# One number of a hand-made order: 16.0 instead of 3.0 matmul-microseconds of projections ahead of the indexer's scores

## The chip, the cores and the metric

The program runs on one core of a Trainium2 chip. The metric is the device time of one execution in microseconds (us). Before the change three runs were timed; one more execution was profiled.

## The reference, cut to what matters

One mixer layer with a mixture of experts, then two layers of a second block; all in float32, on 512 tokens of 1024 features. The change touches the mixer of the first layer alone. There one projection gives the queries of two attentions (`qa`, `qb`), the indexer's queries and key (`qi`, `ki`), keys, values and two gates.

```python
proj = jnp.einsum('bsd,dc->bsc', h, w_in)
qa, ka, va, qi, ki, wi, qb, kvb, gb, gate_a, gate_b = jnp.split(proj, SPLIT_POINTS, axis=-1)
# indexer: eight heads of 32, only tokens it selects are seen by the first attention
idx_logit = jax.nn.relu(jnp.einsum('bthd,bsd->bths', qi, ki))
score = jnp.einsum('bth,bths->bts', wi, idx_logit)
_, sel = lax.top_k(score, k_sel)
o_a = dsa_attention(qa, k, v, sel)                  # softmax over the selected tokens
# second attention: compressed, selected and window branches, weighted by gates
o_b = gc * o_cmp + gs * o_slc + gw * o_win          # queries qb and rope(qb)
merged = jax.nn.sigmoid(gate_a) * (o_a @ w_br_a) + jax.nn.sigmoid(gate_b) * (o_b @ w_br_b)
```

## The kernel before, in words

Matrix products are made of passes on TensorE. A float32 matrix is split into a high and a low part (`wh`, `wl` for weights, `hTh`, `hTl` for the normed tokens), and a step of 128 rows of the contraction is three passes of 512 columns: `hTh,wh`, `hTl,wh`, `hTh,wl`. A product of 128 output columns has eight steps, so 24 passes. The queries `qb` are four products, `qa` four, the gates sixteen.

Weights are fetched by SyncE (a DMA of 512 KB into a raw tile `wr`; line 568 for `qb` and `qa`, line 261 for others), then split: ScalarE writes `wh` (line 242), VectorE or GpSimd `wl` (line 245). A load of `qa` or `qb` serves two products with half of the contraction, so that two loads make two products.

The results of `qb` go through DRAM. `sink` takes a pair of products (two halves of the heads): the pair as it is goes to `d_qn`, and rotated by position (`rope`: four products `t` on VectorE, lines 548 to 551, and a difference and a sum on GpSimd, lines 553 and 554) to `d_qr`. `put` splits each of these four tiles into a high part `sh` (ScalarE, line 534) and a low part `sl` (line 535; VectorE for `d_qn`, GpSimd for `d_qr`) and has SyncE write both (line 540). `sh` and `sl` have two buffers each, so that every third one waits until a write of the tile two before it has landed:

```python
hi = rt.tile([128, T], F32R, tag="sh", name="sh", bufs=2)
lo = rt.tile([128, T], F32R, tag="sl", name="sl", bufs=2)
```

The indexer makes 24 scores (three tiles of tokens, eight heads): a matmul of the index keys `KI` with the index queries `QI` (line 136, as every matmul), a relu `r` on ScalarE (line 779, two buffers) and a weighted sum `sc` on VectorE (lines 781 and 784). `QI` and `KI` are read back from DRAM (lines 637 to 641). Then come `compress` (the products `k_cmp` and `v_cmp`, their blocks `z` against `w1`) and the attentions, sixteen units of a kind and a tile of tokens: S3 W3 C3, S2 W2 C2, S1 W1 C1, S0 W0 C0 of the second attention, D3 D2 D1 D0 of the first (which need the masks `MK` that VectorE makes by `top_k`). Each unit has a part q (scores by query, `KA,QA` and `KC,QB`), a short part b, and a part k (scores by key, `QA,KA`, exponentials, and the sum `po`). Units overlap: part k of one stands behind part q of the next but one.

The order in which all this is emitted is set by `weave`. It walks a chain (indexer, compress, attentions) and takes pieces of a fill (token projections, products of `qb`, of `qa`, of the gates, a step of three passes at a time) between the steps of the chain. The chain can yield a number of microseconds of matmul time as owed to the fill, or a pair (key, lag): then fill is taken until the running sum of matmul time (`self.pe`, 0.425 ns a column, so 0.65 for a step) stands lag behind the moment at which the key was marked. When the chain has ended, what is left of the fill is emitted in one go. The token projections mark the key "tok", and the indexer begins with such a pair:

```python
yield "tok", TUNE["tl0"]
```

The framework's scheduler then lays the instructions out on the engines; each engine runs its own in order, waiting where one isn't ready. SyncE's queue of DMAs is such an order too.

Of the kernel before, what the change touches and what calls it, by code (L numbers as in the profile page):

```python
# [98 lines left out]
    return c  # L99


TUNE = {"mq": 4,"u1":2,"m3":2.0,"m4": 2.0,"m5":1.0,"la":99,"sq2":3.0,"sq":3.0,"fg":2.0,"qt3": 0.5,"bl":2.0,"ee":3,"mk":3.0,"tp":1,"qt1": 1.0,"qt2":1.0,"ws1":1,"ws2":1,"fn": 2.5, "rv": ("qi", "ki"), "tl0": 3.0, "pl": 4.0, "wl": 2.0, "rl": 5.0, "ql": 2.5, "lgm": 8, "shb": 2, "st": 6.0, "sb": 2, "head": 1, "ou": 1, "e2": 3, "p2": 3, "late2": 4, "hv": 0, "pp": 0, "cr": 0, "fp": 2.0, "sh2": 0.0, "mid": 6, "m2": 2.8, "qe": "sync", "y0": {("S", 3): 10.0}, "sh1": 0.5, "cq": 2.5, "o1": [3, 2, 1, 0], "o2": [3, 2, 1, 0], "ix": 0.7, "late": 4, "eb": 3, "ev": 4, "at": 0.5, "tk": 0.0, "tl": 3.0, "obn": 15, "tl2": 1.5, "pf": 3.0, "rx": 4.0, "rs": 6.0, "lo": 16, "lw": 6, "pf0": 2.0, "fx": (0,0,2,0)}


class Kernel:
# [48 lines left out]
    def weave(self, chain, fill, ratio):  # L154
# [14 lines left out]
        for need in chain:  # L169
# [6 lines left out]
            elif need is not None:  # L176
# [8 lines left out]
                owed -= self.pe - p0  # L185
                if TUNE["cr"] == 0 and owed < 0:
                    owed = 0.0
# [70 lines left out]
    def wtile(self, src, kn, cols):  # L258
# [9 lines left out]
        for i in range(0, kn, kn // n):  # L268
            a = slice(i, i + kn // n)
            self.split(hi[:, a], lo[:, a], raw[:, a], hi_eng=eng and (self.nc.vector, None)[TUNE["hv"]], lo_eng=eng)  # L270
        return hi, lo
# [23 lines left out]
    def step(self, k):  # L295
        if k == TUNE["la"]:
            self.due()
# [122 lines left out]
    def first_norm(self, hT, b1, ix):  # L420
# [6 lines left out]
        def load(t):  # L427
            nc.sync.dma_start(xs[t // 2][:, t % 2], I["x"][0, t * 128:(t + 1) * 128])

        def norm(t):  # L430
            x = xs[t // 2][:, t % 2]
            with self.tc.high_priority():
                ss = ix.tile([128, 1], F32, tag="rn_s", name="rn_s", bufs=2)
                nc.scalar.activation(gj[:, 1 + t % 2], x, AF.Square, accum_out=ss)
                rs = self.rstd(ix, ss, 1.0 / D, 1e-6, t == 1)
                nc.vector.scalar_tensor_tensor(x, x, rs, gj[:, 0], op0=OP.mult, op1=OP.mult)
            return lambda: self.to_T(x, hT[0], hT[1], t)

        def rest():
            for t in (2, 3):  # L440
                load(t)
                self.later(TUNE["fn"] * (t - 1), lambda t=t: norm(t)(), t)
        load(0)
# [36 lines left out]
    def mixer1(self, hT):  # L480
# [4 lines left out]
        self.done = {}  # L485
        self.share = TUNE["sh1"]
        pers, pclose = self.pool("b1p")
# [35 lines left out]
        def put(x, n, f, row, rows, ts, scale=None, src0=0, eng=nc.vector):  # L523
# [15 lines left out]
            for x, y in ((0, h), (1, l)):  # L539
                puts.append(self.after(TUNE["pl"], lambda x=x, y=y: nc.sync.dma_start(  # L540
                    DR[n][x, f, row:row + rows, ts], y.bitcast(F32))))
# [1645 lines left out]
```

## Time and profile before

| | us |
|---|---|
| median of three runs | 2065.29 |
| lowest and highest run | 2062.99, 2070.3 |
| the profiled execution's own time | 2065.98 |
| its span, first to last instruction | 2064.2 |
| TensorE busy in it | 1943.5 (94%) |
| longest wait of TensorE | 14.83, ending at 85.32 |
| first matmul of an attention (S3) | 170.76 |
| first matmul of unit D2 | 351.78 |
| last matmul of the attentions | 416.14 |

Times in the trace are microseconds from the span's start. The work around the change lies between 64.84, where the first product of `qb` starts, and some 416, where the attentions end; the remaining three quarters of the span (the merge of the branches, the experts, the second block) come after it and are not touched.

### The profile page before, as it was taken

How to read it: one execution, taken by the hardware profiler on the slowest of the kernel's cores; microseconds unless marked ns; L12 is line 12 of the kernel's file. 1: busy time of each engine (PE TensorE's matmuls, PEld its weight loads, DVE VectorE, ACT ScalarE, POOL GpSimd, SP SyncE). 2: the span in 40 equal slices, each digit the busy share in tenths (PEclk: the TensorE clock that was granted, in tenths of full speed). 3: DMA queues.
4: the chain of work that ended last, by engine and by line, in shares of the span. 5: the costliest groups of instructions: out<-in, count | busy, mean ns of one | idle time of the engine just before them, and what ended most of it. 6: DMA issues, size and time to landing. Idle time of an engine off the chain costs nothing.

```text
span 2064.2 us, 25772 instructions
## 1 busy us (share of the span) xinstructions
PE 1943.5 (94%) x9430; PEld 1521.7 (74%) x9430; DVE 1128.4 (55%) x2034; ACT 844.6 (41%) x1623; POOL 223.1 (11%) x186
## 2 busy tenths in 40 slices
PE   7789989999899998899899999999799999999998
PEld 6667778777555543777778888888687778888886
DVE  8687997664521213687984333335587983333234
ACT  5355657633312112576833222212476833323220
POOL 3143111042000101101020000001001010000001
PEclk9899999999999999899999999999999999999999
DMA  7666433377799995734433333433744334333332
GB/s 188 140 181 147 116 80 103 105 223 275 265 356 395 396 388 183 220 98 128 118 116 111 101 93 102 153 102 108 180 118 128 106 122 150 96 98 96 115 100 71
DMA packets 284495, 328.68 MB, mean 159 GB/s; under 512 B 25562, under 2 KB 206842, under 8 KB 284112
## 3 DMA queue, kind: packets, MB, share of 16 engines
q1 hardware_dynamic: 276912, 306.54, 47.4%
q0 software_dynamic: 7456, 20.49, 3.8%
q8 instruction: 75, 1.23, 0.2%
q14 instruction: 52, 0.43, 0.1%
HBM read 286.63 MB, written 43.38 MB: 160 GB/s over the span
## 4 chain that ended last, share of the span: by engine, by line
PE 52%; DMA 3%; DVE 3%; ACT 2%; issue 1%; POOL 0%; SPq 0%; POOLq 0%; ACTq 0%; DVEq 0%
PE b L136 48%; PE po L136 3%; DVE nm L1891 1%; DMA ks<-bnc 1%; DMA wr<-in_w_in_dram 1%; DMA bnc<-sl 1%; ACT b L1892 1%; PE tp L413 0%; DMA wr<-in_w_o_dram 0%; DMA qs<-bnc 0%; DVE wl L245 0%; DVE pl L245 0%; DMA wr<-in_c_seq_dram 0%; ACT e L1955 0%; ACT wh L242 0%
## 5 line engine op out<-in xcount | busy, mean ns | idle before, releaser
L136 PE MATMUL b<-hTh,wh 128*128 128x512 f32 (+1 forms) x1256 | 477.0, 381 | 7.0 <-ACT wh L242 3.7
L136 PE MATMUL b<-hTh,wl 128*128 128x512 f32 (+1 forms) x1256 | 473.1, 377 | 5.5 <-DVE wl L245 3.4
L136 PE MATMUL b<-hTl,wh 128*128 128x512 f32 (+1 forms) x1256 | 473.6, 377 | 1.7 <-DVE hTl L417 1.7
L242 ACT ACTIVATE wh<-wr 128x1024 fp32r<-128x1024 f32 (+1 forms) x217 | 220.7, 1020 | 561.2 <-PE b L136 332.5
L245 DVE TENSOR_TENSOR wl<-wr,wh 128x1024 fp32r<-128x1024 f32 (+1 forms) x207 | 256.2, 1239 | 340.2 <-ACT wh L242 339.8
L136 PEld LDWEIGHTS b<-hTh,wl 128*128 128x128 f32 x1256 | 240.8, 192 | 50.9 <-DVE wl L245 4.7
L136 PEld LDWEIGHTS b<-hTh,wh 128*128 128x128 f32 x1256 | 241.3, 193 | 50.3 <-ACT wh L242 4.6
L136 PEld LDWEIGHTS b<-hTl,wh 128*128 128x128 f32 x1256 | 241.2, 192 | 41.5 <-DVE hTl L417 3.8
L136 PE MATMUL b<-wl,ah 128*128 128x512 f32 x352 | 137.1, 390 | 0.0
L136 PE MATMUL b<-wh,ah 128*128 128x512 f32 x352 | 137.0, 389 | 0.0
L136 PE MATMUL b<-wh,al 128*128 128x512 f32 x352 | 136.9, 389 | 0.0
L396 POOL TENSOR_TENSOR rs_r<-rs_v,mhalf 128x1 f32<-128x1 f32 x20 | 26.7, 1333 | 781.0 <-DVE rs_v L392 781.0
L245 DVE TENSOR_TENSOR pl<-e,ph 128x512 fp32r<-128x512 f32 x132 | 99.3, 756 | 13.8 <-ACT ph L242 11.4
L1730 DVE TENSOR_TENSOR gs<-b,gs 128x512 f32<-128x512 f32 (+1 forms) x48 | 31.0, 646 | 138.3 <-PE b L136 138.3
L1892 ACT ACTIVATE b<-b,nm 128x512 f32<-128x512 f32 x128 | 84.7, 668 | 23.9 <-DVE nm L1891 23.4
L1891 DVE TENSOR_REDUCE nm<-b 128x1 f32<-128x512 f32 x128 | 82.4, 682 | 18.8 <-PE b L136 18.6
L136 PE MATMUL b<-xr,X 128*64 128x512 f32 x264 | 75.0, 628 | 4.5 <-ACT X L1424 4.5
L136 PEld LDWEIGHTS b<-wl,ah 128*128 128x128 f32 x352 | 66.1, 188 | 13.8
L136 PEld LDWEIGHTS b<-wh,ah 128*128 128x128 f32 x352 | 66.1, 188 | 13.7
L136 PEld LDWEIGHTS b<-wh,al 128*128 128x128 f32 x352 | 66.1, 188 | 13.6
L1955 ACT ACTIVATE e<-b 128x512 f32<-128x512 f32 x128 | 70.6, 616 | 11.5 <-PE b L136 7.4
L245 POOL TENSOR_TENSOR wl<-wr,wh 128x1024 fp32r<-128x1024 f32 (+1 forms) x27 | 55.9, 2073 | 168.3 <-DVE wh L244 80.9
(479 smaller groups left out, 3463.0 us busy)
## 6 DMA issues: line engine op xcount, KB each, us to landing
wr<-in_w_gu_dram SPq DMA_DIRECT2D x88, 512.0 KB
xr<-in_w_gate_up_dram SPq DMA_DIRECT2D x66, 512.0 KB
wr<-in_w_in_dram SPq DMA_DIRECT2D x60, 512.0 KB
wr<-in_w_down_dram SPq DMA_DIRECT2D x44, 512.0 KB
xw<-in_w_gate_up_dram SPq DMA_DIRECT2D x37, 512.0 KB
xy<-in_w_gate_up_dram SPq DMA_DIRECT2D x25, 512.0 KB
xr<-in_w_down_dram SPq DMA_DIRECT2D x24, 512.0 KB
xw<-in_w_down_dram SPq DMA_DIRECT2D x23, 512.0 KB
```

What stands on the lines that cost most here:

```text
L136: self.nc.tensor.matmul(out, a, b, start=start, stop=stop)
L242: nc.scalar.activation(hi, src, AF.Copy)
L245: (lo_eng or nc.vector).tensor_sub(lo, src, hi.bitcast(F32))
L396: nc.gpsimd.tensor_tensor(r, v, self.mhalf, op=OP.pow)
L1730: nc.vector.tensor_mul(g, ps, g)
L1891: nc.vector.tensor_reduce(nm[:, i, r:r + 1], ps, axis=AX.X, op=OP.max, negate=True)
L1892: nc.scalar.activation(ps, ps, AF.Exp, bias=nm[:, i, r:r + 1], accum_out=z[:, i, r:r + 1])
L1955: nc.scalar.activation(e, ps, AF.Exp)
```

## The change

A single entry of the table of numbers changes, and it is used in one place, the line of the indexer shown above:

```diff
-TUNE = {..., "rv": ("qi", "ki"), "tl0": 3.0, "pl": 4.0, ...}
+TUNE = {..., "rv": ("qi", "ki"), "tl0": 16.0, "pl": 4.0, ...}
```

The number is the lag behind "tok". At 0.65 a step, 3.0 is reached in 5 steps and 16.0 in 25; so twenty more steps of `qb`, two and a half products, are emitted ahead of the first score. Since everything else is taken from the fill as before, each later point of the chain stands behind more of the fill, and the fill ends earlier.

What the scheduler makes of it shows in the order on the engines. **First place: TensorE at the first scores.** Before, the first product of `qb` (`b_769`) is followed by three scores, and the second product (`b_809`) is then laid between the scores, one step after each:

```order
L136 MATMUL b_769<-hTh_82,wl_755 128x512
L136 MATMUL b_785<-KI_587,QI_586 128x256
L136 MATMUL b_796<-KI_587,QI_586 128x256
L136 MATMUL b_804<-KI_587,QI_586 128x256
L136 MATMUL b_809<-hTh_82,wh_754 128x512
L136 MATMUL b_809<-hTl_83,wh_754 128x512
L136 MATMUL b_809<-hTh_82,wl_756 128x512
L136 MATMUL b_813<-KI_587,QI_586 128x256
```

Now all four products of `qb` (`b_769`, `b_794`, `b_865`, `b_894`) come first. Behind the last step of the fourth stand seven scores in a row, and then a step of `b_1000`, the first product of `qa`, with weights of `wh_984` and `wl_986`:

```order
L136 MATMUL b_894<-hTh_82,wl_852 128x512
L136 MATMUL b_898<-KI_587,QI_586 128x256
L136 MATMUL b_909<-KI_587,QI_586 128x256
L136 MATMUL b_917<-KI_587,QI_586 128x256
L136 MATMUL b_925<-KI_587,QI_586 128x256
L136 MATMUL b_933<-KI_587,QI_586 128x256
L136 MATMUL b_941<-KI_587,QI_586 128x256
L136 MATMUL b_949<-KI_587,QI_586 128x256
L136 MATMUL b_1000<-hTh_82,wh_984 128x512
L136 MATMUL b_1000<-hTl_83,wh_984 128x512
L136 MATMUL b_1000<-hTh_82,wl_986 128x512
L136 MATMUL b_1004<-KI_587,QI_586 128x256
```

So 72 passes moved from among and behind the scores to a place ahead of them, and the remaining 17 scores now lie among products of `qa`.

**Second place: the writes of `qb` and the first weights of `qa`.** On ScalarE, before, one `sh` of the first product stood ahead of the relus and the next came after ten of them. Now it reads from the sixth relu on (`t_827`, `t_829` and `t_962` are rotated queries, `b_865` and `b_894` the third and fourth product, `wr_988` the first load of `qa`):

```order
L779 ACTIVATE r_943<-b_941 128x256
L779 ACTIVATE r_951<-b_949 128x256
L534 ACTIVATE sh_839<-t_827 128x512
L534 ACTIVATE sh_845<-t_829 128x512
L534 ACTIVATE sh_954<-b_865 128x512
L534 ACTIVATE sh_958<-b_894 128x512
L534 ACTIVATE sh_974<-t_962 128x512
L242 ACTIVATE wh_984<-wr_988 128x512
L242 ACTIVATE wh_985<-wr_988 128x512
```

And on SyncE, after the reads of `KA` and `KC` that stand there in both kernels, the writes and loads are now:

```order
L540 DMA d_qn_178<-sh_819 128x512
L540 DMA d_qn_178<-sl_820 128x512
L540 DMA d_qn_178<-sh_823 128x512
L540 DMA d_qn_178<-sl_824 128x512
L540 DMA d_qr_177<-sh_839 128x512
L540 DMA d_qr_177<-sl_840 128x512
L540 DMA d_qr_177<-sh_845 128x512
L540 DMA d_qr_177<-sl_846 128x512
L540 DMA d_qn_178<-sh_954 128x512
L568 DMA wr_988<-in_w_in_dram 128x4x256
L540 DMA d_qn_178<-sl_955 128x512
L540 DMA d_qn_178<-sh_958 128x512
```

The load `wr_988`, the first of `qa`, stands between the writes of the second pair of `qb`; before, it stood behind all eight writes of `d_qn`, four of `d_qr`, and the loads for `k_cmp`, `v_cmp` and a quarter of `w1`, and TensorE came to the product that needs it later, behind `k_cmp`. The split `wh_984` of `qa` stands behind the seven relus and five of the `sh`.

**Third place: TensorE from D2 to D1.** Before, steps of the gates (`b_3593`) lie between the parts of the units. Here are the last two heads of part q of D2, with a step between them, and its part b:

```order
L136 MATMUL b_3578<-MK2_153,identr_70 128x384
L136 MATMUL b_3593<-hTh_82,wh_3588 128x512
L136 MATMUL b_3593<-hTl_83,wh_3588 128x512
L136 MATMUL b_3593<-hTh_82,wl_3589 128x512
L136 MATMUL b_3597<-KA_144,QA_3518 128x384
L136 MATMUL b_3597<-KC_145,QB_3523 128x384
L136 MATMUL b_3597<-MK2_153,identr_70 128x384
L136 MATMUL b_3603<-identr_70,b20_1438 66x128 x4
```

Now the last gate (`b_3604`) ends ahead of D2, and between the last head, part b and part k of C0 (`KAc`, `KCc` are compressed keys) no step is left:

```order
L136 MATMUL b_3668<-MK2_153,identr_70 128x384
L136 MATMUL b_3677<-KA_144,QA_3608 128x384
L136 MATMUL b_3677<-KC_145,QB_3613 128x384
L136 MATMUL b_3677<-MK2_153,identr_70 128x384
L136 MATMUL b_3683<-identr_70,b20_1547 66x128 x4
L136 MATMUL b_3708<-QA_3355,KAc_164 128x512
L136 MATMUL b_3708<-QB_3360,KCc_165 128x512
L136 MATMUL b_3708<-cmk_162,identr_70 128x512
```

Counted over the whole order, the passes of products that stand ahead of the first matmul of `k_cmp` are 96 before and 153 now; ahead of the first attention 279 and 339; ahead of D2 552 and 624, which is all of them. The fill's last 72 passes, which lay from D2 on, have moved ahead of it.

## Rows read from the trace of the kernel before

**Rows 1.** TensorE's timeline: start, us, engine, line, operation, tiles [idle before <-releaser].
```profile
64.84 0.40 PE L136 MATMUL b<-hTh,wh 128*128 128x512 f32 x1
...
70.10 0.39 PE L136 MATMUL b<-hTh,wl 128*128 128x512 f32 x1
85.32 0.98 PE L136 MATMUL b<-KI,QI 96*128 96x256 f32 x3 [14.83 <-DMA QI<-d_qi]
86.10 0.63 PE L136 MATMUL b<-hTh,wh 128*128 128x512 f32 x1
...
90.58 0.52 PE L136 MATMUL b<-hTh,wh 128*128 128x512 f32 x1
```

**Rows 2.** Windows: us, busy of PE, PEld, DVE, ACT, POOL, PEclk, DMA share, GB/s.
```profile
110.56:170.76 60.20, 53.88 (x224) 41.77 (x225) 43.50 (x67) 26.64 (x43) 30.08 (x23) 0.91 0.67 179
170.76:351.78 181.02, 169.72 (x866) 138.99 (x864) 159.21 (x408) 114.87 (x288) 29.48 (x20) 0.96 0.44 109
351.78:416.36 64.58, 59.97 (x286) 49.32 (x286) 44.07 (x93) 46.26 (x112) 6.78 (x6) 0.92 0.36 104
```

**Rows 3.** TensorE's timeline at k_cmp.
```profile
110.56 0.50 PE L136 MATMUL b<-hTh,wh 128*128 128x512 f32 x1 [1.98 <-ACT wh L242]
...
112.41 0.63 PE L136 MATMUL b<-hTh,wh 128*128 128x512 f32 x1
```

**Rows 4.** ScalarE's timeline: splits of weights, a relu, a split of queries.
```profile
49.34 0.63 ACT L242 ACTIVATE wh<-wr 128x512 fp32r<-128x512 f32 x1 [0.60 <-DMA wr<-in_w_in_dram]
...
92.52 0.38 ACT L779 ACTIVATE r<-b 128x256 f32<-128x256 f32 x1 [0.42 <-PE b L136]
...
104.34 0.62 ACT L534 ACTIVATE sh<-t 128x512 fp32r<-128x512 f32 x1
...
118.43 1.06 ACT L242 ACTIVATE w<-wr 128x1024 fp32r<-128x1024 f32 x1 [2.72 <-DMA wr<-in_w_k_dram]
```

**Rows 5.** VectorE's timeline: a split that waits for a write, a weighted sum, a split.
```profile
52.65 0.86 DVE L538 SCALAR_TENSOR_TENSOR sl<-t,sh 128x256 fp32r<-128x256 f32 x1 [0.57 <-DMA d_k<-sl]
...
88.25 0.48 DVE L781 SCALAR_TENSOR_TENSOR sc<-r,wi,sc 128x256 f32<-128x256 f32 x1 [0.37 <-ACT r L779]
...
95.61 0.69 DVE L535 TENSOR_TENSOR sl<-b,sh 128x512 fp32r<-128x512 f32 x1 [0.18 <-ACT sh L534]
```

**Rows 6.** GpSimd's timeline: rotation and splits of queries.
```profile
97.59 1.29 POOL L553 TENSOR_TENSOR t<-t 128x512 f32<-128x512 f32 x1 [36.56 <-DVE t L549]
...
120.96 3.00 POOL L535 TENSOR_TENSOR sl<-t,sh 128x512 fp32r<-128x512 f32 x2 [0.49 <-DMA d_qn<-sl]
```

**Rows 7.** SyncE's queue: when DMAs were issued.
```profile
45.74 0.38 SPq L568 DMA_DIRECT2D wr<-in_w_in_dram  x1
...
49.91 0.34 SPq L540 DMA_DIRECT2D d_k<-sl  x1
...
111.79 2.23 SPq L717 DMA_DIRECT2D wr<-in_w_k_dram  x1
...
114.74 0.38 SPq L540 DMA_DIRECT2D d_qn<-sl  x1
```

**Rows 8.** Windows of the passes hTl,wh (a third of the fill's) from D2 on.
```profile
351.78:365.20 13.42, 3.14 (x8) 1.00 0.33 89
365.20:384.74 19.54, 3.13 (x8) 0.99 0.54 163
384.74:416.36 31.62, 3.37 (x8) 0.84 0.26 75
```

**Rows 9.** TensorE's timeline ahead of D0.
```profile
384.74 0.45 PE L136 MATMUL b<-KA,QA 128*128 128x128 f32 x1 [2.77 <-DMA QA<-d_qa]
```

**Rows 10.** Windows of all engines in three stretches from D2 on, columns as in rows 2.
```profile
353.20:361.80 8.60, 8.37 (x46) 6.92 (x44) 6.10 (x14) 8.03 (x23) 0.95 (x1) 1.00 0.37 108
...
368.50:379.00 10.50, 10.50 (x48) 8.31 (x47) 8.12 (x19) 10.26 (x25) 0.00 (x0) 1.00 0.46 143
...
396.50:412.50 16.00, 16.00 (x73) 12.96 (x72) 10.38 (x22) 11.81 (x22) 0.00 (x0) 0.95 0.03 10
```

More of the change, by code (lines that the diff above doesn't have):

```diff
@@ L99, in constants @@
     return c
-TUNE = {"mq": 4,"u1":2,"m3":2.0,"m4": 2.0,"m5":1.0,"la":99,"sq2":3.0,"sq":3.0,"fg":2.0,"qt3": 0.5,"bl":2.0,"ee":3,"mk":3.0,"tp":1,"qt1": 1.0,"qt2":1.0,"ws1":1,"ws2":1,"fn": 2.5, "rv": ("qi", "ki"), "tl0": 3.0, "pl": 4.0, "wl": 2.0, "rl": 5.0, "ql": 2.5, "lgm": 8, "shb": 2, "st": 6.0, "sb": 2, "head": 1, "ou": 1, "e2": 3, "p2": 3, "late2": 4, "hv": 0, "pp": 0, "cr": 0, "fp": 2.0, "sh2": 0.0, "mid": 6, "m2": 2.8, "qe": "sync", "y0": {("S", 3): 10.0}, "sh1": 0.5, "cq": 2.5, "o1": [3, 2, 1, 0], "o2": [3, 2, 1, 0], "ix": 0.7, "late": 4, "eb": 3, "ev": 4, "at": 0.5, "tk": 0.0, "tl": 3.0, "obn": 15, "tl2": 1.5, "pf": 3.0, "rx": 4.0, "rs": 6.0, "lo": 16, "lw": 6, "pf0": 2.0, "fx": (0,0,2,0)}
+TUNE = {"mq": 4,"u1":2,"m3":2.0,"m4": 2.0,"m5":1.0,"la":99,"sq2":3.0,"sq":3.0,"fg":2.0,"qt3": 0.5,"bl":2.0,"ee":3,"mk":3.0,"tp":1,"qt1": 1.0,"qt2":1.0,"ws1":1,"ws2":1,"fn": 2.5, "rv": ("qi", "ki"), "tl0": 16.0, "pl": 4.0, "wl": 2.0, "rl": 5.0, "ql": 2.5, "lgm": 8, "shb": 2, "st": 6.0, "sb": 2, "head": 1, "ou": 1, "e2": 3, "p2": 3, "late2": 4, "hv": 0, "pp": 0, "cr": 0, "fp": 2.0, "sh2": 0.0, "mid": 6, "m2": 2.8, "qe": "sync", "y0": {("S", 3): 10.0}, "sh1": 0.5, "cq": 2.5, "o1": [3, 2, 1, 0], "o2": [3, 2, 1, 0], "ix": 0.7, "late": 4, "eb": 3, "ev": 4, "at": 0.5, "tk": 0.0, "tl": 3.0, "obn": 15, "tl2": 1.5, "pf": 3.0, "rx": 4.0, "rs": 6.0, "lo": 16, "lw": 6, "pf0": 2.0, "fx": (0,0,2,0)}
 class Kernel:
```

## The prediction, made before the run

> **What bounds the kernel now.** I began with the page's busy shares: TensorE is busy 94% of the span, so time can come from its waits and from its clock, not from the amount of work, which the change leaves alone. The grouped waits of TensorE came next, and the longest of the program lies at the place that the change touches. In TensorE's timeline the first product of `qb` runs from 64.84 to its 24th pass at 70.10, and then TensorE stands for 14.83 us until `QI` has landed at 85.32 [rows 1]. The passes behind that wait take 0.63 each where those ahead of it took 0.39 to 0.40: the 9 passes from 86.10 up to 90.58 lie 0.42 to 0.43 apart, not 0.229 = (70.10 - 64.84)/23, and the one at 90.58 is the last that is long, 0.52 [rows 1]. That is the lower of the clock's two levels, 1.2 for 2.4 GHz, and costs 9 x 0.2 and some 0.5 for the scores among them and that last one, 2.3 us. I call this a slow restart. So the hole costs 17.1 us in all.
>
> Last I read windows for three stretches behind it [rows 2]: from `k_cmp` to the first attention TensorE waits 60.20 - 53.88 = 6.3 us, from there to D2 11.3, from D2 to the attentions' end 4.6. The last is small because 72 passes of gates lie there, 24 in each third (8 of the pass `hTl,wh`, which is every third of the fill's) [rows 8].
>
> **The change part by part.** It only moves passes. The sum therefore goes by waits that vanish, waits that appear, and cover that is missing.
>
> *The hole at 70 closes.* Four products start at 64.84 and run on: 64.84 + 96 x 0.2287 = 86.8, which is 1.5 us behind the landing of `QI` (the reads stand where they stood). TensorE no longer waits there: -14.8, and -2.3 for the slow restart.
>
> *A hole opens behind seven scores.* Three scores took 0.78 at the low clock (86.10 - 85.32) [rows 1], so seven take some 0.9 at the high one, and at 87.7 TensorE stands at `b_1000`, which needs `wh_984`. What is late is read from the two orders of the second place.
> - Relus: `r` has two buffers, so ScalarE runs at the pace of the sums, 0.48 each [rows 5]. First sum at 87.3, five done by 89.7, the seventh relu, 0.38 [rows 4], ends at 90.1.
> - `sh_839` and `sh_845`, 0.62 each [rows 4], end at 90.7 and 91.3. GpSimd's two `sl` take 3.00 together [rows 6], from 90.7 to 93.7.
> - SyncE issues the write of `sl_846` at 93.7. `sl_959` needs that buffer. From issue to the next use such a write took 52.65 - 49.91 = 2.7 in one place and 120.96 - 114.74 = 6.2 in another [rows 5 to 7]: landed 96.4 to 99.9.
> - `sl_959` 0.69 and one product `t` on VectorE of about the same 0.69 [rows 5], the difference on GpSimd 1.29 [rows 6], `sh_974` 0.62, `wh_984` 0.63 [rows 4]: TensorE can start at 100.3 to 103.8.
> - The load runs beside this. `wr_988` is queued on SyncE behind the write of `sh_954`, which needs the buffer of `sh_839`, written from 90.8: landed 93.5 to 97.0, split 0.6, issue 0.4, so the load starts at 94.5 to 98.0. A load of 512 KB took 49.34 - 45.74 = 3.6 or 118.43 - 111.79 = 6.6 from issue to use [rows 4, 7]: there at 98.1 to 104.6, and with `wh_984` at 98.7 to 105.2.
>
> The later of the two chains gives 100.3 at best and 105.2 at worst. No row is nearer to this case than the others, so I take the middle, 102.8. The hole is then 102.8 - 87.7 = 15.1 us (12.6 to 17.5). It is as long as the old one, so the slow restart comes back too: +15.1 and +2.3.
>
> The Trainium skill ("DMA: Bandwidth & Descriptors", section on the anatomy of one DMA, fitted there on GpSimd's path) gives a DMA about 2.0 us fixed and its bytes at 436 GB/s; by that a write of 256 KB would land in an estimated 2.6 us and a load in 3.2, the hole would end at 100.2, and the sum below would be 2.6 us smaller. The rows here agree with it at their lower ends only, 2.7 and 3.6, and go to more than twice that [rows 4 to 7].
>
> *On to the first attention.* By the counts in the order `k_cmp` has 57 more passes ahead of it, 57 x 0.2287 = 13.0, and then TensorE would reach it 13.0 + 0.3 later. The wait of 1.98 on its weights [rows 3] has no cause left (its weights have 13 us more to be split), nor has the slow restart behind it, 8 passes of 0.63 as the one at 112.41 [rows 3], 8 x 0.2 = 1.6. Until the attention another 3 passes are ahead, 0.7. The other waits of that stretch, 6.3 us, come from splits of `v_cmp`, `w1` and `qa` that follow each other as before; I leave them. First attention: 170.76 + 13.0 + 0.3 - 3.6 + 0.7 = 181.2, that is +10.4, with 13.7 us of work more behind it.
>
> *From there to D2* 12 more passes, 2.7 us, with 11.3 us of waits, a little of which they may fill: +2.0 (0 to 2.7).
>
> *From D2 on* the 72 passes are gone, -16.4 if nothing else bounded that stretch. But they were cover. The third from 351.78 to 365.20: ScalarE is busy 8.03 of 8.60 us from 353.2 to 361.8 [rows 10], so only the ten passes behind that pay, some 2.2 of 5.5 us. The middle third: twelve passes from 368.5 to 379, where ScalarE is full, 10.26 of 10.50 [rows 10], pay nothing, and the other twelve lie right ahead of a wait of 2.77 for D0's queries [rows 9], which are read behind a write of D3's result; they pay nothing, and the wait grows from 2.77 to 5.5. The last third, 396.5 to 412.5: TensorE full, ScalarE 11.81 and VectorE 10.38 of 16.00 [rows 10], so at most 16.0 - 11.8 = 4.2 of the 5.5 can pay. Sum -6.4 (-3 to -10): 10.0 us of cover turn into waits.
>
> *Sum:* +10.4 + 2.0 - 6.4 = +6.0 against the profiled execution's own 2065.98 (its span of 2064.2 and 1.8 around it, which stay), so 2072.0 on its scale. It lies 0.7 above the median of the runs, so I forecast 2071.3 for the median.
>
> **The rivals.** 0.3% of 2065, 6.2 us, is about what a measurement of this kernel can tell from no change, so my forecast lies on that line.
>
> *The end needs no cover* (not slower). The units from D2 on overlap, and if ScalarE's work slides under TensorE's the stretch gives back all 16.4. For it: from 396.5 no other engine is full. Against: ScalarE is, from 353 to 362 and from 368 to 379. Then 10.4 + 2.0 - 16.4 = -4.0: 2061.3. It decides from the point where 12.4 of the 16.4 come back.
>
> *The weights are there in time* (faster). If the first load of `qa` were issued at some 82, behind the reads of `KC`, and split ahead of the writes, the new hole would fall to under 1 us with no slow restart: 6.0 - 15.1 - 2.3 = -11.4: 2053.9. Against it stand both orders, in which ScalarE can't pass `sh_974` and SyncE can't pass the write of `sh_954`. It becomes the better story from a hole under 4 us on.
>
> *Later weights are late too* (slower still). The loads for `k_cmp` and `v_cmp` now stand behind both pairs of `qa` in SyncE's queue. If one of them isn't there, TensorE waits up to a load, 6.6 [rows 4, 7], and restarts slowly, 2.0: 6.0 + 8.6 = +14.6: 2079.9. Against: they are needed only at some 122, 19 us behind the new hole.
>
> **How the numbers follow.** Forecast as summed 0.55, with a range of its own from 2065 to 2077 (hole 12.6 to 17.5, end -3 to -10); end without cover 0.17; weights in time 0.08; later weights late 0.20. The range to 2080 takes in the last case; downwards it stops at 2059, below the end without cover with the short hole (2061.3 - 2.5), and leaves out the weights in time. Slower by over 0.3%: half of the forecast and most of the last case, 0.28 + 0.18 = 0.46. Within: 0.27 + 0.11 + 0.02 = 0.40. Faster: 0.06 + 0.08 = 0.14.
>
> **What would show it.** In the changed kernel's TensorE timeline: no wait from 64.8 to 86.8; first score at 86.8; a wait of 12.6 to 17.5 behind the seventh score, put down to ScalarE's `wh`, and passes of 0.63 behind it; the attention's first matmul at 181.2; no wait at `k_cmp`; from D2 on waits of some 14.6 us where there were 4.6, that before D0 at 5.5. I would be wrong if the hole is under 10 us, if the stretch from D2 shrinks by more than 12 us, or if new waits over 3 us show between 103 and 181.

## The result, and the profile after

The changed kernel takes 2089.7 us (median of 6, 2083.81 to 2091.59), the kernel before beside it 2065.95; the ratio is 1.0106, 95% interval 1.0086 to 1.0125. It is slower, as forecast, but by three to four times as much as the 6.0 us of the sum, and above the range. The profiled execution is one of its faster ones, 2084.69, 18.7 us above the one of before; the stretches below are of these two.

| stretch | before | after | difference | forecast |
|---|---|---|---|---|
| start to first score | 85.32 | 85.86 | +0.5 | +1.5 |
| to the first attention | 85.4 | 100.2 | +14.7 | +8.9 |
| to D2 | 181.0 | 184.6 | +3.6 | +2.0 |
| to the first product of the merge | 64.6 | 72.1 | +7.5 | -6.4 |
| to the first product of an expert | 129.3 | 120.4 | -8.9 | 0 |
| to the end | 1518.6 | 1519.7 | +1.1 | 0 |

The stretches are cut at TensorE's timeline. Where the first score, the hole, the first attention, and the waits between stand in the timeline of after answers to [rows 1, 3]:

```profile
85.86 1.14 PE L136 MATMUL b<-KI,QI 96*128 96x256 f32 x7
101.25 0.80 PE L136 MATMUL b<-hTh,wh 128*128 128x512 f32 x1 [14.25 <-ACT wh L242]
...
129.74 0.64 PE L136 MATMUL b<-hTh,wl 128*128 128x512 f32 x1 [2.99 <-POOL wl L245]
141.90 1.22 PE L136 MATMUL b<-w,z 128*128 128x256 f32 x8 [2.56 <-DVE z L706]
154.23 0.50 PE L136 MATMUL b<-hTh,wh 128*128 128x512 f32 x1 [1.93 <-ACT wh L242]
166.69 0.30 PE L136 MATMUL b<-ce,w 128*64 128x62 f32 x2 [2.63 <-issue]
...
186.03 0.39 PE L136 MATMUL b<-KA,QA 128*128 128x512 f32 x1
```

The old hole is gone and the new one is there, behind the seven scores, 14.25 us long; the forecast said 15.1. Behind it are four waits of 2 to 3 us; with smaller ones they make 13.2 us of waits up to the first attention, where the forecast left 6.3. The windows of after, columns as in [rows 2]:

```profile
121.00:186.03 65.03, 52.45 (x226) 40.91 (x225) 45.70 (x58) 24.32 (x36) 28.07 (x19) 0.95 0.51 145
186.03:370.67 184.64, 172.26 (x878) 138.56 (x877) 159.51 (x404) 112.83 (x287) 23.73 (x16) 0.98 0.37 93
370.67:442.80 72.13, 48.69 (x214) 39.14 (x213) 45.88 (x94) 61.94 (x128) 11.93 (x12) 0.79 0.42 117
370.67:443.26 72.59, 49.15 (x216) 39.52 (x215) 46.34 (x95) 61.94 (x128) 11.93 (x12) 0.79 0.42 117
```

In the third of them, from D2 to the merge, TensorE has 72 instructions less than before (214 for 286), and yet the stretch is longer: 23.4 us of waits where there were 4.6, at a mean clock of 0.79 for 0.92. The fourth window ends at the attentions' last pass, for this reason: in both kernels the first product of the merge stands ahead of that pass. Before, the attentions don't end at 416.14, as the front of this document and the prediction have it. One more `po` pass comes at 420.68, with a wait ahead of it that lies behind every stretch of the sum:

```profile
420.68 0.50 PE L136 MATMUL po<-pl,VS 128*128 128x512 f32 x1 [3.69 <-DVE pl L245]
351.78:420.68 68.90, 60.60 (x288) 49.51 (x287) 48.39 (x94) 47.98 (x113) 11.09 (x10) 0.93 0.40 115
```

(The first line is TensorE's timeline of before, the second a window of it.) One `pl` of VectorE takes 4.82 us there, its two neighbours 0.68; why is not shown. So from D2 to the attentions' last pass it is 68.9 us before and 72.6 after, +3.7, and 3.8 of the +7.5 in the table come from where the stretch is cut.

ScalarE is the engine that gained: 61.94 us busy for 46.26, in 16 instructions more. Its timeline shows which:

```profile
377.45 1.28 ACT L1072 ACT_TABLE_LOAD   x1
378.74 0.63 ACT L1072 ACTIVATE g<-g 128x512 f32<-128x512 f32 x1
379.39 1.28 ACT L233 ACT_TABLE_LOAD   x1
380.68 0.21 ACT L233 ACTIVATE le<-lz 128x8 f32<-128x8 f32 x1
...
383.05 1.28 ACT L1072 ACT_TABLE_LOAD   x1
384.35 0.63 ACT L1072 ACTIVATE g<-g 128x512 f32<-128x512 f32 x1
...
387.72 1.28 ACT L926 ACT_TABLE_LOAD   x1
...
395.15 1.28 ACT L231 ACT_TABLE_LOAD   x1
...
396.67 1.28 ACT L993 ACT_TABLE_LOAD   x1
```

Line 1072 is the sigmoid of the gates, in the code that merges the branches. Before, all sixteen ran from 416 on, behind one table load. Now the gates' products end ahead of D2, their results are in DRAM early, and the scheduler lifted ten sigmoids with their reads in among the attentions' exponentials. A sigmoid needs another table of functions than an exponential or a logarithm, and each change back and forth is a table load of 1.28 us: ten of them from 377.45 to 424.60, 12.8 us. TensorE's timeline names who waits for it:

```profile
382.57 0.79 PE L136 MATMUL po<-ph,Vc 128*128 128x512 f32 x1 [5.63 <-ACT ph L242]
...
399.72 0.79 PE L136 MATMUL po<-ph,VS 128*128 128x512 f32 x1 [2.31 <-ACT ph L242]
411.26 0.45 PE L136 MATMUL b<-KA,QA 128*128 128x128 f32 x1 [5.82 <-DMA QA<-d_qa]
...
427.44 0.79 PE L136 MATMUL po<-ph,VS 128*128 128x512 f32 x1 [4.43 <-ACT ph L242]
```

Each of the three waits for `ph` ends behind a pair of table loads. The one for D0's queries grew from 2.77 [rows 9] to 5.82; the prediction had 5.5.

The table loads stood in the order on ScalarE before the kernel ran, though the front of this document doesn't show that place:

```order
L231 ACTIVATE lz_3698<-z_3618 128x8
L1072 ACT_TABLE_LOAD
L1072 ACTIVATE g_4281<-g_4281 128x512
L233 ACT_TABLE_LOAD
L233 ACTIVATE le_3700<-lz_3698 128x8
L993 ACTIVATE e_3712<-b_3708 128x512
```

### The profile page after: what moved, and what is told of

Read it like the earlier page. It is cut to its first block, busy times and chain, and to the rows that moved or that the text cites. A ratio compares the mean times of both kernels' runs of the same rounds, so it can differ in the third digit from the quotient of the medians.

```text
span 2082.9 us, 25770 instructions
## 1 busy us (share of the span) xinstructions
PE 1945.4 (93%) x9430; PEld 1521.4 (73%) x9430; DVE 1132.5 (54%) x2034; ACT 856.9 (41%) x1633; POOL 225.1 (11%) x186
## 4 chain that ended last, share of the span: by engine, by line
PE 49%; DMA 4%; DVE 4%; ACT 2%; issue 1%; SPq 0%; POOLq 0%; DVEq 0%; ACTq 0%
PE b L136 45%; PE po L136 3%; DMA ks<-bnc 1%; DMA wr<-in_w_in_dram 1%; DVE nm L1891 1%; ACT b L1892 1%; DMA bnc<-sl 1%; DVE wl L245 1%; DMA wr<-in_w_o_dram 1%; PE tp L413 0%; ACT wh L242 0%; ACT e L1955 0%; DMA qs<-bnc 0%; DVE e L1957 0%; DVE pl L245 0%
## 5 line engine op out<-in xcount | busy, mean ns | idle before, releaser
L136 PEld LDWEIGHTS b<-wh,al 128*128 128x128 f32 x352 | 66.1, 188 | 13.8
L136 PEld LDWEIGHTS b<-wh,ah 128*128 128x128 f32 x352 | 66.1, 188 | 13.7
L136 PEld LDWEIGHTS b<-wl,ah 128*128 128x128 f32 x352 | 66.1, 188 | 13.6
```

Of the source, the lines that this page charges most:

```text
L136: self.nc.tensor.matmul(out, a, b, start=start, stop=stop)
```

## The experiments

All ratios are against the kernel before on the same chip. Names of theories in the expectations: theory 1 is that the loss lies at the end, in table loads; theory 2 that the new hole is the chain of writes of `qb`; theory 3 that the fill is wanted at the end and not ahead of D2; theory 4 concerns GpSimd.

**Sigmoids held behind the attentions (pin16).** One edit notes the attentions' last copy on ScalarE, the other queues the sigmoids behind it:

```diff
-                    nc.scalar.activation(t, po[64:128], AF.Copy)
+                    self.last_act = nc.scalar.activation(t, po[64:128], AF.Copy).ins
...
-            nc.scalar.activation(g, g, AF.Sigmoid)
+            with self.tc.issue_after(self.last_act): nc.scalar.activation(g, g, AF.Sigmoid)
```

> The changed kernel, with the sigmoids of the gates held behind the last ScalarE instruction of the attentions, so that none of the ten table loads (1.28 us each in the changed kernel's trace) lies among the attentions. The fill is the changed kernel's, so no cover is put back. Theory 1 (the table loads and the ten sigmoids made the end long): the stretch from D2 to the end of the attentions falls from 72.8 us to 57 to 63, the wait of 5.6 ahead of C0's part and that of 4.4 ahead of D0's last go, and the time falls to 2074 to 2083, since the sigmoids come back behind the attentions. Rival (the missing cover alone made it long, the table loads lay in its shade): the stretch stays at 70 or more and the time at 2088 to 2098.

2082.55 us, 1.0056 (1.0038 to 1.0074): 7 us below the changed kernel's median, inside the range, at its upper end. Its windows from D2 to the merge and to the attentions' last pass:

```profile
375.05:440.65 65.60, 48.56 (x215) 38.83 (x214) 43.86 (x94) 44.02 (x108) 12.26 (x12) 0.82 0.46 128
375.05:441.11 66.06, 49.02 (x217) 39.20 (x216) 44.32 (x95) 44.02 (x108) 12.26 (x12) 0.82 0.46 129
```

65.6 us, 6.5 less than with the early sigmoids, and 66.1 to the attentions' last pass (second line), also 6.5 less. That is not the 57 to 63 that was expected: with 72 passes less than the kernel before, the stretch up to the last pass is only 2.8 shorter than there. The two waits that were to go only shrink, from 5.63 to 2.06 and from 4.43 to 1.74. So theory 1 holds for the table loads. The rest of the stretch is bound by no single engine: ScalarE is busy 44.02 of 65.60, TensorE 48.56, and TensorE's longest waits are 5.72 for D0's queries and 4.62 for a `pl` of VectorE.

**A copy in place of the sigmoid (copy16).** `AF.Copy` for `AF.Sigmoid` in that line. The output is another one; only the times are of use.

> The changed kernel with a plain copy in place of the gates' sigmoid (the output is another one for that). The copies stay where the scheduler likes them, among the attentions, but need no other table, so the ten table loads go and the moved work of 0.57 us each stays. Two ways to read the 6.5 us that the held sigmoids gave back between D2 and the router's first transposition (141.1 to 134.6). Table loads themselves: that stretch is 133 to 137 and the time 2074 to 2082. The moved sigmoids, as work among the attentions: 139 or more and 2085 or more.

The stretch from D2 to the router's first transposition, behind all products of the merge, is 134.0 (139.4 before, 141.5 in the changed kernel, 134.9 with held sigmoids), the one to the merge 64.0:

```profile
371.48:435.44 63.96, 45.98 (x214) 37.03 (x213) 43.84 (x94) 48.49 (x118) 12.28 (x12) 0.84 0.48 134
```

So it is the loads, not the ten moved instructions; ScalarE is busy 13.45 us less than with them (61.94 - 48.49). The time, 2085.0, 1.0078 (1.0054 to 1.0101), lies above the 2074 to 2082 of the table loads and at the bound of the other reading; by itself it tells neither, since its interval overlaps those of the changed kernel and of the held sigmoids.

**Table loads in the kernel before (tab3).** `tl0` is 3.0 here, so the fill stands at the end as before.

```diff
             QA, QB = rows.pop((kind, i))
+            if kind == "D" or (kind, i) == ("C", 0):
+                self.tc.keep_in_program_order(nc.scalar.activation(dummy[0], dummy[0], AF.Sigmoid))
```

> The kernel before with five sigmoids of a small tile (128 x 8, used by nothing) at the heads of the parts k of C0, D3, D2, D1 and D0, so that twelve table loads lie among the attentions' end, 15.4 us of ScalarE, while the fill still has 72 passes there. Theory 1 (ScalarE's chain sets the length of that stretch, so a table load costs time wherever the fill stands): from D2 to the first product of the merge 70 to 76 us where it was 64.2, time 2073 to 2081. Rival (the table loads hurt only where the cover is gone): 66 or less, time within 4 of the kernel before.

2084.7 us, 1.0082 (1.0053 to 1.011), 17.2 above the kernel before. The sigmoids themselves take 0.21 each; what they bring is the loads, fourteen of them and not the twelve that were expected (ScalarE has 19 instructions more than before in the window, 5 of them the sigmoids). ScalarE's timeline at one of the five shows four, and TensorE's 72 passes more don't hide them in the window:

```profile
376.69 1.28 ACT L231 ACT_TABLE_LOAD   x1
...
378.21 1.28 ACT L233 ACT_TABLE_LOAD   x1
379.51 0.21 ACT L233 ACTIVATE le<-lz 128x8 f32<-128x8 f32 x1
379.73 1.28 ACT L954 ACT_TABLE_LOAD   x1
381.03 0.21 ACT L954 ACTIVATE dummy<-dummy 128x8 f32<-128x8 f32 x1
381.25 1.28 ACT L998 ACT_TABLE_LOAD   x1
```

```profile
355.04:437.46 82.42, 64.03 (x286) 50.93 (x286) 44.09 (x93) 64.73 (x131) 9.20 (x9) 0.89 0.31 89
```

82.4 us for 64.6: fourteen loads, 17.9 us of ScalarE, lengthen the stretch by 17.8, 1.3 each, more than the 70 to 76 that was expected. Up to the attentions' last pass it is 84.6 for 68.9, 1.1 each. So at the heads of the parts k cover doesn't hide a table load: it costs about its whole length. The ten of the changed kernel, 12.8 us, cost less, 6.5 to 8.2 (pin16 and copy16 against the changed kernel, latepin against late), so not all of their length was waited for; what hid the rest is not shown. What the fixed place of the five sigmoids in the order costs beside their loads was not run apart.

**The early products without the early end (cover16).** `"ix": 0.16` for 0.7 beside `"tl0": 16.0`: the scores owe less to the fill.

> The early products without the early end: tl0 is 16.0 as in the change, and ix, the time that each of the 24 scores owes to the fill, falls from 0.7 to 0.16, so that by the order the fill stands as before from the compressed products on, with 72 passes behind D2 and no sigmoid among the attentions. Theory 1 (the loss lies at the end, the new hole only takes the old one's place): from D2 to the end 64 to 66 us as before, and the time at 2058 to 2068. Rival (the loss lies at the front, where the order of scores and products starves TensorE): the first attention starts at 178 or later, where it was 170.8, and the time is 2074 or more.

2070.5 us, 1.0011 (0.9994 to 1.0028): no difference from the kernel before that the runs can tell; the median is 2.5 above the range, the runs of the kernel before beside it stood 2.2 above its first median. First score to first attention 85.9 (85.4 before), D2 to the merge 62.6. The hole has only moved again, to the first weights behind the 24 scores:

```profile
112.98 0.79 PE L136 MATMUL b<-hTh,wh 128*128 128x512 f32 x1 [13.78 <-ACT wh L242]
```

So putting four products ahead of the scores neither gains nor loses; what loses is that everything behind came earlier in the fill.

**The early end without the early products (late, latepin).** `"ix": 1.24` with `"tl0": 3.0`, without and with the held sigmoids.

> The early end without the early products: tl0 is 3.0 as before, and ix rises from 0.7 to 1.24, so that the scores begin as before with the wait of 14.8 us for QI, and the fill runs out ahead of D2 as in the changed kernel, with ten sigmoids among the attentions. Theory 1 (the loss lies at the end): from D2 to the end 70 to 75 us, time 2080 to 2092, as the changed kernel. Rival (loss at the front, by the products moved ahead of the scores): from D2 to the end below 66 us, time 2060 to 2072.

> As the kernel with tl0 3.0 and ix 1.24, with the sigmoids held behind the attentions. What is left against the kernel before is the price of the missing cover alone. Theory 1: from D2 to the end 57 to 63 us, time 2070 to 2080, that is 8 or more below the same kernel without the hold. Rival (the missing cover is the price): within 4 of the same kernel without the hold.

2091.56, 1.0103 (1.0087 to 1.0119), as the changed kernel, though its scores begin as those of before. With held sigmoids 2089.72, 1.0096 (1.0077 to 1.0115). The two windows from D2 to the merge are 71.31 and 64.56 (first line without the hold, second with it), as in the other pair:

```profile
380.22:451.53 71.31, 50.10 (x215) 40.44 (x213) 46.29 (x94) 61.54 (x128) 11.93 (x12) 0.76 0.44 118
```

```profile
377.21:441.77 64.56, 47.01 (x214) 37.66 (x213) 43.89 (x94) 43.94 (x108) 12.28 (x12) 0.84 0.47 131
```

The medians are only 1.8 apart, where the windows promise 6.8 and 8 was expected; the executions of either kernel spread by 8, so this pair's times don't confirm what its traces show. The larger part of the loss in both is ahead of the first attention: 107.8 and 107.3 us from the first score on, 22 more than before for 13.7 us of products. The expectation that the loss lies at the end alone is wrong here, and so is that of 57 to 63 us at the end.

**Cover taken from the middle (at16_30).** `"at": 0.3` for 0.5 beside `"tl0": 16.0`.

> The early products as in the change, but the share of fill that the attentions owe falls from 0.5 to 0.3, so that 72 passes stand behind D2 again, taken from the stretch between the first attention and D2, and no sigmoid lies among the attentions. Theory 3 (the end needs the 72 passes as cover and the stretch ahead of D2 does not): D2 to the end 63 to 67 us as before, first attention to D2 168 to 172 where it was 185, time 2066 to 2074. Rival (cover is worth the same in both): first attention to D2 stays at 180 or more, time 2082 or more.

2086.44 us, 1.0093 (1.0062 to 1.0124); no sigmoid among the attentions. Its windows, from the first attention to D2, from there to the merge, and the last part of that, with the wait ahead of D0 from TensorE's timeline between them:

```profile
188.25:366.75 178.50, 160.63 (x806) 128.63 (x804) 157.86 (x403) 111.04 (x284) 20.41 (x15) 0.95 0.35 89
366.75:437.78 71.03, 60.92 (x287) 49.89 (x286) 47.96 (x104) 47.27 (x113) 8.86 (x6) 0.90 0.35 103
403.94 0.45 PE L136 MATMUL b<-KA,QA 128*128 128x128 f32 x1 [6.06 <-DMA QA<-d_qa]
431.65:437.78 6.13, 6.13 (x28) 5.07 (x27) 4.21 (x11) 3.33 (x5) 0.00 (x0) 1.00 0.39 123
```

By its time theory 3 falls: taking 72 passes, 16.4 us, out of the first stretch shortens it by only 6.1 (184.6 to 178.5), so that some 10 of them were cover there, and the second is 5.4 longer than with the held sigmoids (65.6 to 71.0). But the edit did not do all that was meant. The attentions' last pass is at 431.41, and 27 of the 72 passes, 9 steps, run behind it, in the last window, where there is nothing of the attentions left to cover. The other 45 cost nothing: up to the last pass it is 64.7 us, with the held sigmoids and none of them 66.1. So by this comparison the fill is full cover among the last attentions as far as it stands there; what all 72 would give there with the fill of the changed kernel ahead the run doesn't show. Up to the router's first transposition the kernel is 9.9 behind the one with held sigmoids (144.8 for 134.9); 4.4 of that arise in the merge, and their cause was not looked for.

**The new hole (qa16pin).** The first two loads of `qa` are emitted when the third product of `qb` begins, with the sigmoids held:

```diff
+            def third():
+                got = two[0]()
+                if n == "qb":
+                    ready["qa"] = pair_tiles(W_IN["qa"], 64, ("qa", 0))
+                    ready["qa"][0]()
+                return got
```

> The changed kernel with the sigmoids held behind the attentions, and with the first two loads of qa's weights emitted ahead of the writes of the rotated queries, so that they stand on SyncE's queue before the write of sh_839 and their splits right behind it. Theory 2 (the hole behind the seven scores is the chain of writes through sh and sl that the load and its split stood behind): the hole falls from 15.1 to between 3 and 7 us, the stretch from the first score to the first attention from 102 to 90 to 95 us, the time to 2070 to 2077. Rival (the hole is the load itself or ScalarE's own work, whatever stands ahead): hole still over 10 us. Second rival: the hole closes but later waits take it back, stretch still 99 or more.

2076.2 us, 1.0042 (1.0024 to 1.006): the hole falls from 15.1 in the kernel with held sigmoids to 8.8.

```profile
96.89 0.79 PE L136 MATMUL b<-hTh,wh 128*128 128x512 f32 x1 [8.79 <-ACT wh L242]
```

```profile
88.12 1.89 SPq L568 DMA_DIRECT2D wr<-in_w_in_dram  x2
```

The second fence is SyncE's queue: the loads were issued at 88.12, 1.2 us behind the first score, where it had been 10.6, and ScalarE's first split could begin at 96.21. So the chain of writes was in the way, as theory 2 has it, but the hole is longer than 3 to 7, since the two loads take 8 us, and of the 6.3 us won only 4 arrive at the first attention (102.2 to 98.2, outside the 90 to 95; the waits for `wl` and `z` behind the hole go on).

**Early loads with the cover in place (kc16, kc3, kc11, kc16g).** The same place in the emission, but with the weights that come next there, those of `k_cmp` and `v_cmp`: `kv.extend(f() for f in self.columns(w, [W_IN["k_cmp"], W_IN["v_cmp"]]))`. kc16 has `tl0` 16.0 and `ix` 0.16, kc3 the 3.0 and 0.7 of before, kc11 11.0 and 0.375; kc16g is kc16 with these loads on GpSimd's queue.

> The kernel with tl0 16.0 and ix 0.16 (cover at the end as before), with the weights of k_cmp and v_cmp loaded ahead of the writes of the rotated queries. Theory 2: its hole of 13.8 us ahead of k_cmp falls to 4 to 8, the first attention starts at 163 to 168, time 2059 to 2066, below the kernel before. Rival (later waits take it back, on z, w1 or qa): first attention at 171 or later, time 2067 or more.

> The kernel before (tl0 3.0, ix 0.7) with the early loads for k_cmp and v_cmp alone. If the gain of the version with tl0 16.0, ix 0.16 and the same early loads (0.997 of the kernel before) comes from the loads alone: 0.994 to 0.998 here too. If it takes the products ahead of the scores as well, since only they open a hole for the loads to close: 0.999 to 1.002.

> tl0 11.0 and ix 0.375 with the early loads of k_cmp and v_cmp: three products ahead of the scores, the fourth among them, fill as before from the compressed products on. Theory 2: TensorE waits some 4 us for QI at 81, the fourth product fills the hole of 6.1 us ahead of k_cmp that four products ahead leave: first attention 80 to 83 after the first score, time 2055 to 2062, as good as or better than the version with 16.0. Rival (the two waits add up): 2063 to 2068.

> tl0 16.0, ix 0.16 and the loads for k_cmp and v_cmp on GpSimd's queue in place of SyncE's, so that no write stands ahead of them; the split of k_cmp's weights then stands ahead of the relus on ScalarE. Theory 2: the hole ahead of k_cmp, 6.1 us with the loads on SyncE, goes, as does the restart at the low clock behind it; first attention 4 to 8 us earlier against the first score than the 82.9 there; time 2052 to 2060. Rival: the two loads, 1 MB at 71 to 80, stand in the way of QI, and the first score comes 2 to 5 us later: no gain, 2060 to 2066.

kc16 takes 2061.26 us, 0.997 (0.9949 to 0.9992), the only version here that is faster than the kernel before. Its hole ahead of `k_cmp` is 6.08 for 13.78, and from the first score to the first attention it takes 82.9 us, 2.5 less than before (the attention itself starts at 172.2, outside the expected 163 to 168 and by the letter where the rival had it, 171 or later: in that execution the first score came late, at 89.28):

```profile
107.78 0.80 PE L136 MATMUL b<-hTh,wh 128*128 128x512 f32 x1 [6.08 <-ACT wh L242]
```

The loads alone (kc3) give 2065.67, 0.9991 (0.9975 to 1.0008), nothing that can be told from no change. The products alone (cover16) gained nothing either, so it seems to take both, the products to fill the first hole and the loads to fill the second; but the intervals of kc16 and kc3 overlap, and that the products are needed is not shown by the times. Three products (kc11) give 2062.89, 0.9984 (0.9966 to 1.0003); its interval covers that of kc16 and no change, and both of its holes are there, 8.76 and 4.79:

```profile
90.12 4.37 PE L136 MATMUL b<-KI,QI 96*128 96x256 f32 x13 [8.76 <-DMA QI<-d_qi]
108.83 0.80 PE L136 MATMUL b<-hTh,wh 128*128 128x512 f32 x1 [4.79 <-ACT wh L242]
```

On GpSimd's queue (kc16g) it is 2071.25, 1.0013 (0.9997 to 1.003). The hole ahead of `k_cmp` goes, but one of 12.8 us, ending at 127.2, opens ahead of `qa`; neither expectation had that, and its cause was not looked for.

**GpSimd's split (vdve16).** In the kernel with held sigmoids the low part of `v_cmp`'s weights is made by VectorE.

> The changed kernel with held sigmoids, and the low part of v_cmp's weights made by VectorE in place of GpSimd. In the changed kernel TensorE waits 3.0 us at 129.7 for it. Theory 4 (GpSimd is late because the rotation and splits of qb stand ahead on it): that wait falls under 1 us, first attention 2 to 3 us earlier against the first score, 99 to 100.5. Rival (VectorE is as late): the wait changes its name, or the next one, for z, grows by as much, 101.5 to 104. The time alone, 2079 to 2083, can't tell it.

The wait of 3.07 for GpSimd is gone, and that for `z` on VectorE grew from 2.47 to 5.65:

```profile
144.75 1.65 PE L136 MATMUL b<-w,z 128*128 128x256 f32 x6 [5.65 <-DVE z L706]
```

The rival holds in the main: the next wait takes it over. The first attention comes 1.6 us earlier, 100.6 after the first score, between the two expectations; the time is 2084.88, 1.0069 (1.0042 to 1.0096), above the 2079 to 2083 and not to be told from the held sigmoids.

**Both together (qaat30).** The early loads of `qa` with `"at": 0.3`.

> Both together: early products, early loads of qa's weights, and 72 passes behind D2 by the share of 0.3. If theories 2 and 3 hold it is faster than the kernel before by 4 to 12 us, 2054 to 2062. If only one holds, 2064 to 2074.

2078.04 us, 1.0058 (1.0037 to 1.0078), slower than either expectation and no faster than the early loads of `qa` alone (2076.2). One of its 13 executions took 6921 us, the others 2071 to 2087; that one was profiled, so no trace of this kernel is read, and why it gains nothing stays open.

## Why the prediction was wrong

By its own steps:

- *The hole at 70 closes.* Right: no wait from 64.8 to the first score at 85.86.
- *A hole opens behind seven scores.* Right in mechanism, and in size partly by luck: 14.25 for 15.1, and the start at 101.25 for 102.8. The chain is in ScalarE's timeline of after:

```profile
91.43 0.63 ACT L534 ACTIVATE sh<-t 128x512 fp32r<-128x512 f32 x1 [1.61 <-DMA d_qn<-sh]
...
100.05 0.63 ACT L534 ACTIVATE sh<-t 128x512 fp32r<-128x512 f32 x1 [3.18 <-POOL t L553]
100.59 1.13 ACT L242 ACTIVATE wh<-wr 128x512 fp32r<-128x512 f32 x2
```

  The split `wh` stands behind `sh_974`, which waits for GpSimd's rotation, as worked out. A term was missing, the wait for the write of `sh_819` at 91.43, and the last write that counts (issued at 94.69, its buffer in use at most 2.7 later) landed at the lower end of its range. The two offset each other; the middle of the range, for which no row spoke, came out for that reason.
- *On to the first attention.* Wrong in size, by 4.8: 186.03 for 181.2 (by 6.4 if counted from the end of the hole, which came 1.6 early). The sum took one wait away, left 6.3 us of the others, and had no new ones. Between the hole and the attention there are 13.2 us of waits. The larger ones are for `wl` of GpSimd (2.99), for `z` of VectorE (2.56), for a split of ScalarE (1.93), and one (2.63) for which the trace names nothing: the helpers, not TensorE, set the pace in most of them, and vdve16 shows a wait going from one helper to the next. What part of them each helper causes was not settled.
- *From there to D2.* +3.6 for +2.0: the 12 passes, and 1.1 us of waits more where some were to be filled.
- *From D2 on.* This is the step that failed. The forecast was -16.4 for the passes that are gone and +10.0 for waits in their place, -6.4. Up to the attentions' last pass the changed kernel shows +3.7 (68.9 to 72.6). That is -16.4, +15.1 of waits (8.3 to 23.4), and +5.0 because the passes that are left run at a mean clock of 0.79 for 0.93 (they keep TensorE busy for 49.15 us, where 60.60 - 16.4 = 44.2 would be left). Two terms were missing.

  The first is the table loads: the step costed the 72 passes that are gone and not what the scheduler puts in their place. In three pairs of kernels the ten loads account for 6.5 to 8.2 us of that stretch (72.1 against 65.6 and 64.0, 71.3 against 64.6).

  The second is the clock: new waits of TensorE bring slow restarts, which the prediction priced at both holes and put at nothing here. The passes behind the three waits for `ph` above take 0.79, against the usual 0.39 to 0.40. With held sigmoids it is still +4.8.

  The other waits came near in sum, 8.7 for 10.0 with held sigmoids, but not for the reasons given. The vanished wait of 3.69 for the last pass, which the sum didn't know of, is in it. And the wait ahead of D0 has its size (5.82 for 5.5) not just from the twelve passes that are gone: in at16_30 twelve passes stand right ahead of it again, and it is 6.06.

  From D2 to the experts it is 193.8 before, 187.1 with held sigmoids and 192.5 in the changed kernel. The -6.7 without the table loads lies close to the -6.4 of the sum, but by luck: in it are the 3.7 of that wait, 1.6 for the slow passes behind it and 2.3 ahead of the experts, none of them a term of the sum. With the table loads it is -1.3.
- *The sum.* The misses of these terms, 4.8 + 1.6 + 5.1, are 11.5, and 1.1 lie behind the experts' start: 12.6 of the 12.7 between +6.0 and +18.7. Another 5 us, between that execution and the medians (23.8), are spread that no single trace explains.

Of the rivals, "later weights are late too" came nearest, in place and partly in size, but not by its mechanism alone. "The end needs no cover" and "the weights are there in time" didn't come about; qa16pin made the second in part, 8.8 us of hole instead of under 1.

The Trainium skill ("ScalarE: Activation LUTs", section on what ACT_TABLE_LOAD costs) says that a switch of tables is some 1.3 us for the load and with the drain about 2.7; its section on table sets says that calls should be grouped by table. The trace agrees on the load, 1.28, and on the grouping (6.5 us for ten loads between exponentials); it doesn't on the drain: at 378.74 the sigmoid starts 0.01 behind the load's end, and tab3 gives 1.3 us for each switch, drain and all.

## What to carry to other kernels

When work is moved ahead, ask what its results set free: a consumer far behind may become ready, and a scheduler that goes by readiness will lift it into a place where it costs more than it is worth. Read the whole new order on every engine for instructions that appear, table loads above all, and not only for those that moved; here they stood in it. A hole that closes tells nothing until the weights behind it are followed through the queue: with four products ahead of the scores the hole only moved, and it took an earlier load as well (0.997 of the kernel before) to gain from it. And cut a stretch at an instruction that has the same work ahead of it in both orders: the first product of the merge stood ahead of a late pass of the attentions in one kernel and behind nine steps of fill in another, and misled by 4 to 6 us.

## What the runs showed of the hardware

A table load on ScalarE took 1.28 us each time. Fourteen of them at the heads of the parts k made a stretch of 64.6 us 17.8 us longer, though TensorE was busy in it 60.0 of 64.6 us before; ten elsewhere cost about half to two thirds of their length. After a sigmoid, logarithm and exponential, which had run without a load between them, got a load each (376.69 and 378.21 in tab3, 395.15 and 396.67 in the changed kernel), so that one sigmoid of 0.21 us stood among four. Where TensorE's waits grew from 8.3 to 17.0 us in a stretch (before, held sigmoids), its mean clock fell from 0.93 to 0.82, and the passes that both have took some 4.8 us longer. Two 512 KB loads issued together at 88.12 were in use 8.1 us later, more than the 6.6 that a single one took at worst [rows 4, 7].
